# First loads of a batched matmul: one DMA of 8 KB runs for each operand in place of a 2 KB and a 6 KB one

## The chip, the cores and the metric

One core of a Trainium2 chip. The metric is the device time of one launch in microseconds. "Engine" in this document mostly means one of the core's 16 DMA engines; PE, DVE, ACT and SP are the tensor, vector, scalar and sync engines. HBM is the chip's large memory, SBUF the core's working memory, and PSUM holds what PE has summed. A DMA is moved in packets, and "2 KB runs" are stretches of 2 KB that lie together on both sides, one packet each; a run that is timed is one execution. A spread is the highest time less the lowest.

## The reference

```python
batch, m, k, n = 16, 512, 512, 512
a: [batch, k, m] float32      b: [batch, k, n] float32
out = np.matmul(a.transpose(0, 2, 1), b)      # float32
```

33.55 MB come in and 16.78 MB go out.

## The kernel before

Inputs come from HBM into four 2 MB buffers, are cast to bf16 by DVE, multiplied by PE, copied out of PSUM by ACT, and go back to HBM from seven 2 MB output buffers. Loads and stores are all issued by SP, in one order. Batches go in pairs, but the first pair is loaded batch by batch, so that the first matmuls need only 2 MB.

```python
in0_v = [x.rearrange("batch (p r) m -> batch p r m", r=RV) for x in (a, b)]       # RV = 4: 8 KB runs
top_v = [x[0][0:P].rearrange("p m -> p () m") for x in (a, b)]                    # 2 KB runs
low_v = [x[0][P:K].rearrange("(p r) m -> p r m", r=RV - 1) for x in (a, b)]       # 6 KB runs
...
for j in range(2):                                        # first a, first b
    nc.sync.dma_start(x_ts[j][:, 0:1, :], top_v[j]).then_inc(s_f[j], 16)
    nc.sync.dma_start(x_ts[j][:, 1:RV, :], low_v[j]).then_inc(s_f[j], 16)
for j in range(2):                                        # second a, second b
    nc.sync.dma_start(x_ts[j][:, RV:R, :], in0_v[j][1]).then_inc(s_x[j], 16)
for n in range(2, 2 * pairs):                             # all other loads, 2 MB each
    if n >= NX:
        nc.sync.wait_ge(s_in, n - NX + 1)                 # a buffer is free again
    ...
# DVE, first pair
for u in range(G):
    if u:
        nc.vector.wait_ge(s_mm, H)
    for j, bf_ts in enumerate((abf_ts, bbf_ts)):
        nc.vector.wait_ge(s_x[j] if u else s_f[j], 16 if u else 32)
        nc.vector.tensor_copy(out=bf_ts[0][:], in_=x_ts[j][:, u * RV:(u + 1) * RV, :]).then_inc(s_cast, 1)
```

The cast waits for 32 counts: both pieces of a tensor.

Of the kernel before, what the change touches and what calls it, by code (L numbers as in the profile page):

```python
# [8 lines left out]
def kernel(  # L9
# [6 lines left out]
    nc = tc.nc  # L16
    P = 128
    batch, K, M = a.shape
# [11 lines left out]
    RV = R // V  # L30
# [3 lines left out]
    in_v = [x.rearrange("(pair g) (q r) m -> pair (g q) r m", g=G, r=R) for x in (a, b)]  # L34



    in0_v = [x.rearrange("batch (p r) m -> batch p r m", r=RV) for x in (a, b)]
    top_v = [x[0][0:P].rearrange("p m -> p () m") for x in (a, b)]
    low_v = [x[0][P:K].rearrange("(p r) m -> p r m", r=RV - 1) for x in (a, b)]  # L40
    out_v = out.rearrange("(pair g) (c t) n -> pair c g t n", g=G, t=T)

    NX = 4
# [10 lines left out]
    x_ts = [pool.tile([P, R, M], f32, name=f"x{j}") for j in range(NX)]  # L54
# [5 lines left out]
    s_x = [tc.alloc_semaphore(f"s_x{j}") for j in range(NX)]  # L60
    s_f = [tc.alloc_semaphore(f"s_f{j}") for j in range(2)]
# [9 lines left out]

    with tc.tile_critical(no_gpsimd_drain=True):  # L72
        for j in range(2):
            nc.sync.dma_start(x_ts[j][:, 0:1, :], top_v[j]).then_inc(s_f[j], 16)
            nc.sync.dma_start(x_ts[j][:, 1:RV, :], low_v[j]).then_inc(s_f[j], 16)
        for j in range(2):
            nc.sync.dma_start(x_ts[j][:, RV:R, :], in0_v[j][1]).then_inc(s_x[j], 16)
        for n in range(2, 2 * pairs):
            if n >= NX:
                nc.sync.wait_ge(s_in, n - NX + 1)  # L80
            src, x = in_v[n % 2][n // 2], x_ts[n % NX]
# [11 lines left out]
        for u in range(G):  # L93
            if u:
                nc.vector.wait_ge(s_mm, H)
            for j, bf_ts in enumerate((abf_ts, bbf_ts)):
                nc.vector.wait_ge(s_x[j] if u else s_f[j], 16 if u else 32)
                nc.vector.tensor_copy(  # L98
                    out=bf_ts[0][:], in_=x_ts[j][:, u * RV:(u + 1) * RV, :]
                ).then_inc(s_cast, 1)  # L100
                if u == G - 1:
                    nc.vector.memset(dve_done[:, j:j + 1], 0.0).then_inc(s_in, 1)  # L102
# [120 lines left out]
```

## Time and profile before

| | |
|---|---|
| time, median of 3 runs | 123.50 us (123.36 to 123.52) |
| the execution that was profiled | 123.84 us, span 122.1 us |
| bytes moved | 50.33 MB |
| steady rate of the transfers | 427 to 430 GB/s |

The page and the windows of before are shown in the prediction. One thing is added here, the timeline of before at the first two casts (start, length, engine, line, operation; in brackets how long DVE had been idle and what ended it):

```profile
5.82 1.23 DVE L98 CAST abf<-x 128x2048 bf16<-128x2048 f32 x1 [5.82 <-DMA x<-in_a_dram]
8.95 1.23 DVE L98 CAST bbf<-x 128x2048 bf16<-128x2048 f32 x1 [1.91 <-DMA x<-in_b_dram]
```

The bracket of the second says that b's landing released it. So 8.95 us is when the first b was seen to be there.

A second source is used all through: the trace's packet records, with start, duration and size of every DMA packet. Each DMA ends with one 4-byte packet on each of the 16 engines, the semaphore increment. Sorted by time, 16 at a time, they tell when the first and when the last engine got through each DMA. The records do not name the engine: "the last engine" is whichever came last.

### The profile page before, as it was taken

What the parts mean: (1) busy time and instruction counts of PE and PEld (TensorE: products, weight loads), DVE (VectorE), ACT (ScalarE), POOL (GpSimd) and SP (SyncE); (2) the same over time, 40 slices, a digit from 0 to 9 for tenths busy, and PEclk for the clock granted to TensorE, in tenths of its full rate; (3) what the DMA queues carried; (4) which work ended last, traced back from release to release, by engine and by line L of the source; (5) the groups of instructions that cost most, each with busy time, mean ns of one, the idle gap of its engine ahead of it and who ended that gap; (6) DMA issues with size and microseconds to landing.
All of it is one profiled execution on the core that took longest, in us unless ns stands there. A gap on an engine that the chain in (4) does not pass through costs nothing.

```text
span 122.1 us, 1209 instructions
## 1 busy us (share of the span) xinstructions
PE 62.1 (51%) x480; PEld 35.0 (29%) x480; DVE 38.1 (31%) x48; ACT 32.2 (26%) x41; POOL 0.2 (0%) x4
## 2 busy tenths in 40 slices
PE   0005928379969749979919928989900000000000
PEld 0002304035546325636606605646500000000000
DVE  0033070680494092474356437492000000000000
ACT  4000332400570840091470290091570000000000
POOL 0000000000000000000000000000000000000000
PEclk9999999959999985999999999999997555555555
DMA  2999999999999999999999999999999999999993
GB/s 86 375 411 429 454 429 435 435 440 435 429 429 429 429 429 429 429 429 435 429 429 435 429 429 416 421 429 427 427 421 429 427 429 427 429 429 424 427 429 145
DMA packets 5200, 50.33 MB, mean 412 GB/s; under 512 B 464, under 2 KB 464, under 8 KB 976
## 3 DMA queue, kind: packets, MB, share of 16 engines
q1 hardware_dynamic: 5200, 50.33, 97.3%
HBM read 33.55 MB, written 16.78 MB: 412 GB/s over the span
## 4 chain that ended last, share of the span: by engine, by line
DMA 43%; DVE 7%; ACT 3%; PE 3%; issue 3%; ACTq 0%
DMA x<-in_b_dram 37%; DMA out_dram<-o 6%; DVE abf L117 4%; ACT o L180 3%; DVE bbf L117 3%; PE ps L135 3%; DVE done L123 0%; ACTq L72 0%
## 5 line engine op out<-in xcount | busy, mean ns | idle before, releaser
L155 PE MATMUL ps<-bbf,abf 64*128 64x512 bf16 x448 | 52.9, 393 | 13.1 <-PEq L150 13.1
L155 PEld LDWEIGHTS ps<-bbf,abf 64*128 64x128 bf16 x448 | 31.2, 113 | 34.8 <-issue 20.0
L180 ACT COPY o<-ps 128x1024 f32<-128x1024 f32 x28 | 26.3, 1026 | 40.5 <-PE ps L155 36.5
L117 DVE CAST abf<-x 128x2048 bf16<-128x2048 f32 x14 | 17.1, 1224 | 17.4 <-PE ps L155 13.3
L117 DVE CAST bbf<-x 128x2048 bf16<-128x2048 f32 x14 | 17.1, 1225 | 14.2 <-DMA x<-in_b_dram 14.2
L135 PE MATMUL ps<-bbf,abf 128*128 128x512 bf16 x32 | 9.2, 451 | 13.2 <-PEq L133 13.2
L135 PEld LDWEIGHTS ps<-bbf,abf 128*128 128x128 bf16 x32 | 3.8, 123 | 18.1 <-issue 16.1
L174 ACT COPY o<-ps 128x1024 f32<-128x1024 f32 x4 | 4.1, 1014 | 17.2 <-PE ps L135 17.2
L98 DVE CAST abf<-x 128x2048 bf16<-128x2048 f32 x2 | 2.5, 1227 | 11.7 <-PE ps L135 5.9
L98 DVE CAST bbf<-x 128x2048 bf16<-128x2048 f32 x2 | 2.5, 1225 | 1.9 <-DMA x<-in_b_dram 1.9
L185 ACT ACTIVATE done<-done 1x1 uint32<-1x1 uint32 x8 | 1.6, 196 | 0.0
L174 ACT ACT_TABLE_LOAD x1 | 1.3, 1283 | 0.9 <-SPq L72 0.9
L123 DVE MEMSET done<- 1x1 f32 x14 | 0.8, 59 | 0.0
L102 DVE MEMSET done<- 1x1 f32 x2 | 0.1, 59 | 0.0
L207 POOL MEMSET const-bfloat16-1.0<- 128x1 bf16 x1 | 0.1, 102 | 0.0
L207 POOL MEMSET const-uint8-127<- 128x1 uint8 x1 | 0.1, 102 | 0.0
L207 POOL MEMSET const-float32-0.0<- 128x1 f32 x1 | 0.1, 99 | 0.2 <-issue 0.2
L207 POOL MEMSET const-float32-1.0<- 128x1 f32 x1 | 0.1, 99 | 0.0
## 6 DMA issues: line engine op xcount, KB each, us to landing
out_dram<-o SPq DMA_DIRECT2D x8, 2048.0 KB, 21.8
x<-in_a_dram SPq DMA_DIRECT2D x7, 2048.0 KB, 12.1
x<-in_b_dram SPq DMA_DIRECT2D x6, 2048.0 KB, 15.9
x<-in_b_dram SPq DMA_DIRECT2D x3, 1024.0 KB, 13.4
x<-in_a_dram SPq DMA_DIRECT2D x1, 1024.0 KB, 8.6
x<-in_a_dram SPq DMA_DIRECT2D x1, 768.0 KB, 4.4
x<-in_b_dram SPq DMA_DIRECT2D x1, 768.0 KB, 6.6
x<-in_a_dram SPq DMA_DIRECT2D x1, 256.0 KB, 2.8
```

The lines of the kernel that those rows point to most:

```text
L98: nc.vector.tensor_copy(out=bf_ts[0][:], in_=x_ts[j][:, u * RV:(u + 1) * RV, :]).then_inc(s_cast, 1)
L102: nc.vector.memset(dve_done[:, j:j + 1], 0.0).then_inc(s_in, 1)
L117: nc.vector.tensor_copy(out=(bbf_ts if n % 2 else abf_ts)[v][:], in_=x_ts[n % NX][:, v * RV:(v + 1) * RV, :],).then_inc(s_cast, 1)
L123: nc.vector.memset(dve_done[:, n:n + 1], 0.0).then_inc(s_in, 1)
L135: mm = nc.tensor.matmul(ps_ts[0][h][:, t % 2, :], a_m[:, r, t], bbf_ts[0][:, r, :], start=(r == 0), stop=(r == RV - 1),)
L155: mm = nc.tensor.matmul(ps_ts[g][h][:, t % 2, :], a_m[:, t], bbf_ts[v][rows, r, :], start=(v == 0 and r == 0), stop=(v == V - 1 and r == R ...
L174: nc.scalar.copy(out=o_ts[0][:, g, 2 * h:2 * h + 2, :], in_=ps_ts[0][h][:]).then_inc(s_ev[h], 1)
L180: ev = nc.scalar.copy(out=o_ts[i % NO][:, g, 2 * h:2 * h + 2, :], in_=ps_ts[g][h][:])
L185: nc.scalar.memzero(act_done[:, i:i + 1]).then_inc(s_out, 1)
L207: nc = _bacc.Bacc("TRN2", target_bir_lowering=False, num_devices=1)
```

## The change

Its intent: fewer and longer packets at the very start, two DMAs fewer, two increments fewer.

```diff
-    top_v = [x[0][0:P].rearrange("p m -> p () m") for x in (a, b)]
-    low_v = [x[0][P:K].rearrange("(p r) m -> p r m", r=RV - 1) for x in (a, b)]
 ...
         for j in range(2):
-            nc.sync.dma_start(x_ts[j][:, 0:1, :], top_v[j]).then_inc(s_f[j], 16)
-            nc.sync.dma_start(x_ts[j][:, 1:RV, :], low_v[j]).then_inc(s_f[j], 16)
+            nc.sync.dma_start(x_ts[j][:, 0:RV, :], in0_v[j][0]).then_inc(s_f[j], 16)
 ...
-                nc.vector.wait_ge(s_x[j] if u else s_f[j], 16 if u else 32)
+                nc.vector.wait_ge(s_x[j] if u else s_f[j], 16)
```

## The prediction

> **What bounds the kernel now.** I read the page first (busy shares, the 40 slices, the DMA packets), then the waits of the DMA-issuing engine, then tables of short windows over the start and the end, then the timeline of the first 24 us, and last the trace's own packet records.
>
> The page: no compute engine is busy even 55% of the span, the DMA engines are.
>
> ```profile
> span 122.1 us, 1209 instructions
> PE 62.1 (51%) x480; PEld 35.0 (29%) x480; DVE 38.1 (31%) x48; ACT 32.2 (26%) x41; POOL 0.2 (0%) x4
> ...
> DMA  2999999999999999999999999999999999999993
> ...
> DMA packets 5200, 50.33 MB, mean 412 GB/s; under 512 B 464, under 2 KB 464, under 8 KB 976
> q1 hardware_dynamic: 5200, 50.33, 97.3%
> ...
> x<-in_a_dram SPq DMA_DIRECT2D x1, 768.0 KB, 4.4
> x<-in_b_dram SPq DMA_DIRECT2D x1, 768.0 KB, 6.6
> ```
>
> The reader is to see a transfer stream with no hole in it: every slice but the first and last reads 9, and 97.3% is the whole span less about 2.2 us at the start and 1.6 us at the end. So the end is: when the stream starts, plus 50.33 MB at its rate, plus a tail. What the casts and matmuls do matters only if it makes the stream run dry. The packet counts also fit the program: 29 DMAs x 16 = 464 tiny packets (the semaphore increments), and 976 - 464 = 512 packets of 2 or 6 KB, which are the four DMAs of the change (4 x 128).
>
> The windows (length, then engines, granted clock, DMA share, GB/s):
>
> ```profile
> 2.00:2.50 0.50, 0.00 (x0) 0.00 (x0) 0.00 (x0) 0.18 (x1) 0.00 (x0) 1.00 0.45 98
> 2.50:3.50 1.00, 0.00 (x0) 0.00 (x0) 0.00 (x0) 0.00 (x0) 0.00 (x0) 1.00 0.98 342
> 3.50:5.00 1.50, 0.00 (x0) 0.00 (x0) 0.00 (x0) 0.00 (x0) 0.00 (x0) 1.00 1.00 416
> 5.00:6.50 1.50, 0.00 (x0) 0.00 (x0) 0.68 (x1) 0.00 (x0) 0.00 (x0) 1.00 1.00 350
> 6.50:8.00 1.50, 0.00 (x0) 0.00 (x0) 0.54 (x1) 0.00 (x0) 0.00 (x0) 1.00 1.01 421
> 8.00:12.00 4.00, 1.53 (x4) 0.59 (x5) 1.23 (x1) 0.00 (x0) 0.00 (x0) 1.00 1.02 428
> ...
> 40.00:79.00 39.00, 30.19 (x260) 18.34 (x258) 18.94 (x24) 15.28 (x20) 0.00 (x0) 0.96 1.01 430
> 81.00:120.00 39.00, 7.21 (x64) 4.29 (x64) 2.20 (x4) 5.70 (x8) 0.00 (x0) 0.65 1.01 427
> 120.00:120.50 0.50, 0.00 (x0) 0.00 (x0) 0.00 (x0) 0.00 (x0) 0.00 (x0) 0.50 0.28 115
> ```
>
> The last column is the case. The rate is 427 to 430 GB/s everywhere except at two dips, 342 and 350, and these are where the 2 KB runs of a (2.2 to 3.3 us) and of b (5.0 to 6.7 us) go through. The 6 KB runs read 416 and 421; the second batch's 8 KB runs, from about 8 us, already read 428. The DMA share stays at 1.00 in the dips: the engines are not idle, their packets are slow.
>
> **What the Trainium skill says.** (1) "DMA: Bandwidth & Descriptors", section "Why small descriptors are slow (HBM only)", gives each packet a fixed overhead, put at about 3 cycles. The trace agrees that there is a fixed part. Median packet times in its records are 84 ns for 2 KB, 234 for 6 KB, 309 for 8 KB, 611 for 16 KB: from 2 to 8 KB that is 225 ns for 6144 B, so 9 ns fixed and 0.0366 ns a byte, and 6 KB comes out at exactly 234. (2) The same page, "Why a DMA increments its semaphore by 16 and not by 1": every engine that takes part posts one increment after its data. The 464 agree, 9 ns each. (3) "Perfetto Trace Analysis", section "DMA Optimizations", says that splitting into smaller chunks may let some start sooner if the DMA engines are generally idle. Here they are not, and the cast waits for both pieces of the split (32 counts), so nothing in this kernel uses the earlier piece.
>
> **The change, part by part.** It removes four DMAs (two of 256 KB, two of 768 KB) and adds two of 1 MB in the same buffer space; the cast waits for 16 counts instead of 32. Row order inside batch 0 changes for a and b alike, so the sum over k is the same. Casts, matmuls, evictions, outputs: unchanged, at the same durations.
>
> *Issues.* The six first issues stand 0.94 to 3.27 us, 0.47 us apart. Two fewer lets all later ones leave 0.94 us sooner. Worth nothing by itself: the stream is fed from a queue that holds 8.4 MB by 4.7 us.
>
> *Packets.* Each of the 16 engines now moves 2 x 8 packets of 2 KB and 2 x 8 of 6 KB: 16 x 84 + 16 x 234 = 5088 ns, with 4 increments 5124. Then 16 x 309 + 2 x 9 = 4962 ns. Gain 0.16 us, on the path that sets the end, since each engine works through a fixed list.
>
> *Stalls around the short packets.* The 0.16 does not explain the dips. Between 2.5 and 3.5 us the shortfall against 428 is 86 KB, between 5.0 and 6.5 it is 117 KB, and in the two 6 KB windows 18 and 11 KB: 232 KB, or 0.54 us in the mean of the engines. The records show where: at the first 6 KB packets behind the 2 KB ones, around 3.0 us, five packets take 310 to 380 ns longer than their median, and around 5.6 to 5.9 us seven take 180 to 780 ns longer. At the change from one 8 KB DMA to the next, nothing like it: only a few packets 50 to 135 ns over.
>
> *The last engine.* The end is set by the slowest engine, so I follow the increments of each DMA from the first engine's to the last's: top of a 2.95 to 3.35 us, rest of a 4.95 to 5.44, top of b 5.64 to 6.70, rest of b 7.70 to 8.57, second a 10.16 to 11.02. From there on the lag of 0.86 us stays to the nanosecond through all reads, and is still 0.86 at the last increment (119.94 to 120.80). From 8.57 on the last engine thus runs at a fixed pace: 120.80 - 8.57 = 112.23 us, then 1.3 us to the span's end. The span is the last engine's finish of b plus 113.5 us.
>
> So what is wanted is that finish after the change. An 8 KB DMA takes an engine 2.453 us (second a: 8.57 to 11.02). The last engine to start has its first packet near 2.77 us, and a first packet takes some 0.24 us extra (up to 241 ns in the records). 2.77 + 0.24 + 2 x 2.453 = 7.92 us instead of 8.57: 0.65 us less, if no 8 KB packet stalls. If the same engine loses 0.2 us all the same, 0.45. The floor is the 0.16 of packet overhead.
>
> *Sum.* Mechanism alone: 0.16 to 0.65 us, middle about 0.5, so a time near 123.0 from 123.5.
>
> **The rivals.**
> (a) *A slower start with long first runs.* Short first packets may get the engines going sooner; somebody chose 2 KB runs ahead of 6 KB, and as the cast waits for both, nothing else in the kernel gives a reason for it. Against it: the last engine's first packet already comes 0.6 us behind the first one's, which no packet size explains, and the dips are at the short runs. If true, 123.5 to 123.9.
> (b) *The gain is lost behind a wait.* The stream could run dry where a buffer comes free. The issuing engine's waits:
>
> ```profile
> SPq L83 <- DVE done L102: 13.5, 2, 12.7
> SPq L91 <- DMA x<-in_b_dram: 12.6, 1, 12.6
> ```
>
> The first ends at 17.34 us, when the load in front of it still runs until 22.34 on the first engine; with 1.24 us from issue to first packet (0.94 to 2.18 at the start) there are 3.8 us to spare, and the chain to it starts with b's landing, which the change brings forward. The second ends at 79.5; outputs issued then can start at 80.75, just as the first engine is through with the last load at 80.73. Tight, but it is timed by the stream itself and moves along with it; if lag shrinks it gets looser. So this rival costs 0.0, at worst 0.2 us.
> (c) *The earlier start of the casts is worth more.* b's landing (8.95 us, the cast's start) would come about 0.65 sooner, but no compute lies at the end: the last output is issued at 90.84 and lands 30 us later in a queue that is full. Worth 0.
>
> **Range and chances.** The mechanism gives 122.85 to 123.35, middle 123.0; rival (a) at about one in four pulls up. I say 123.1, and 122.6 to 123.7 for 8 in 10: the low end allows 0.9 us, the whole lag of the last engine taken away; the high end a start that costs 0.2. Runs of before lie within 0.16 us, so this is readable. Two per cent is 2.47 us, more than the first 8.6 us can give at all (every engine starting at 2.18 and taking 4.91 us would be through at 7.09, 1.5 us sooner): faster 0.01, same 0.97, slower 0.02.
>
> **What would show it.** In the changed profile: 4912 packets (5200 - 256 - 32), with 432 under 512 B and 432 under 8 KB; two fewer issues; 420 GB/s or more in 3.5 to 8 us with no dip near 5 to 6.5; the cast of b starting near 8.3 instead of 8.95; outputs' last packets near 120.2 and a span near 121.6. The page's rate after 10 us unchanged at 427 to 430. I am wrong in the step "stalls" if a dip or slow packets of 8 KB appear in the first 8 us, wrong in the step "last engine" if b comes in earlier but the end doesn't move with it, and wrong altogether if the first packets come later than 2.2 to 2.8 us.

## The result

| | median | range | runs |
|---|---|---|---|
| before | 123.51 us | 123.36 to 123.54 | 4 |
| after | 123.34 us | 123.17 to 123.40 | 4 |

Ratio 0.9986, 95% interval 0.9969 to 1.0003: the same at 2%. A ratio is the mean time of one kernel's runs over that of the other's in the same rounds, so not quite the ratio of the medians.

The page of after, the lines that answer to those of before:

```profile
span 121.7 us, 1207 instructions
PE 65.0 (53%) x480; PEld 35.6 (29%) x480; DVE 38.0 (31%) x48; ACT 32.2 (26%) x41; POOL 0.2 (0%) x4
...
DMA  3999999999999999999999999999999999999993
...
DMA packets 4912, 50.33 MB, mean 414 GB/s; under 512 B 432, under 2 KB 432, under 8 KB 432
...
q1 hardware_dynamic: 4912, 50.33, 97.8%
...
x<-in_b_dram SPq DMA_DIRECT2D x4, 1024.0 KB, 12.1
x<-in_a_dram SPq DMA_DIRECT2D x2, 1024.0 KB, 6.8
```

4912 packets, 432 of them increments, none left between 512 B and 8 KB. The stream still has no hole. Then the same windows (last columns: granted clock, DMA share, GB/s):

```profile
2.00:2.50 0.50, 0.00 (x0) 0.00 (x0) 0.00 (x0) 0.18 (x1) 0.00 (x0) 1.00 1.26 180
2.50:3.50 1.00, 0.00 (x0) 0.00 (x0) 0.00 (x0) 0.00 (x0) 0.00 (x0) 1.00 0.50 213
3.50:5.00 1.50, 0.00 (x0) 0.00 (x0) 0.00 (x0) 0.00 (x0) 0.00 (x0) 1.00 1.02 426
5.00:6.50 1.50, 0.00 (x0) 0.00 (x0) 0.69 (x1) 0.00 (x0) 0.00 (x0) 1.00 1.03 431
6.50:8.00 1.50, 0.00 (x0) 0.00 (x0) 0.54 (x1) 0.00 (x0) 0.00 (x0) 1.00 1.04 437
8.00:12.00 4.00, 2.21 (x6) 0.88 (x7) 1.23 (x1) 0.00 (x0) 0.00 (x0) 1.00 1.01 426
...
40.00:79.00 39.00, 30.52 (x248) 17.47 (x246) 18.31 (x24) 15.27 (x20) 0.00 (x0) 0.91 1.00 430
```

From 3.5 us on it runs at full rate; the dip at 5.0 to 6.5 (350 GB/s before) is gone. The start, though, is worse: 213 GB/s from 2.5 to 3.5 us where before had 342. The engines' first packets start earlier than before's (1.96 to 2.21 us, before 2.18 to 2.50), but the records give them 0.79 to 1.29 us each in place of 0.31, so the first 8 KB are through near 3 us. The earlier start is not the change's doing: two later profiles of before start at 1.96 and 1.98. b's landing, in the timeline of after:

```profile
5.81 1.23 DVE L94 CAST abf<-x 128x2048 bf16<-128x2048 f32 x1 [5.81 <-DMA x<-in_a_dram]
8.26 1.23 DVE L94 CAST bbf<-x 128x2048 bf16<-128x2048 f32 x1 [1.22 <-DMA x<-in_b_dram]
```

a lands when it did (5.81 and 5.82), b 0.69 us sooner. The waits of the issuing engine, after, against the two of before:

```profile
SPq L79 <- DVE done L98: 14.5, 2, 13.7
SPq L87 <- DMA x<-in_b_dram: 12.6, 1, 12.6
```

The first is longer although b came sooner, because SP was done with its first issues 0.7 us earlier, and because PE's first 16 matmuls took 6.57 us in this execution and 5.55 in that of before, so the first refill left at 17.67 (before 17.34). It cost nothing here.

So the profiles differ by 0.4 us in span (122.1 to 121.7) and 0.69 us in b's landing, the times by 0.17 us. That gap is what the experiments are about.

### The profile page after: what moved, and what is told of

It is laid out like the page before. It is cut to its first block, busy times and chain, and to the rows that moved or that the text cites. A ratio compares the mean times of both kernels' runs of the same rounds, so it can differ in the third digit from the quotient of the medians.

```text
span 121.7 us, 1207 instructions
## 1 busy us (share of the span) xinstructions
PE 65.0 (53%) x480; PEld 35.6 (29%) x480; DVE 38.0 (31%) x48; ACT 32.2 (26%) x41; POOL 0.2 (0%) x4
## 2 busy tenths in 40 slices
DMA packets 4912, 50.33 MB, mean 414 GB/s; under 512 B 432, under 2 KB 432, under 8 KB 432
## 3 DMA queue, kind: packets, MB, share of 16 engines
q1 hardware_dynamic: 4912, 50.33, 97.8%
## 5 line engine op out<-in xcount | busy, mean ns | idle before, releaser
L131 PE MATMUL ps<-bbf,abf 128*128 128x512 bf16 x32 | 11.9, 554 | 12.5 <-PEq L129 12.5
L131 PEld LDWEIGHTS ps<-bbf,abf 128*128 128x128 bf16 x32 | 4.3, 138 | 19.6 <-issue 19.1
```

Source lines behind the costliest of these rows:

```text
L131: mm = nc.tensor.matmul(ps_ts[0][h][:, t % 2, :], a_m[:, r, t], bbf_ts[0][:, r, :], start=(r == 0), stop=(r == RV - 1),)
```

## The experiments

Theories. **P** (packets): only the fixed time of 16 packets and two increments for each engine went away. **S** (stalls): 2 KB runs stall in every execution, and the change removes some 0.4 us of that. **N**: noise. After the first four runs came **V**: a tensor cut into two DMAs lets single engines fall behind by an amount that varies from execution to execution; later told apart as **VC** (the count of DMAs does it), **VA** (the addresses do) and **V2** (b's cut alone does it).

Twelve runs, of nine kernels, were made in three calls, each call on a chip of its own, with other runs of before among them. The changed kernel was not in call 3, so there it is compared across calls. All were correct.

### Call 1: before and after again

Both unchanged; no diff.

> The kernel before, unchanged, timed against itself: a null, and a second profile of it. The first profile of before was taken in an execution of 123.84 us, 0.34 above its median, so it may show more loss than a usual run has. Theory S (stalls behind the 2 KB runs are what the change removes, 0.4 us of it): ratio 1.000, and the new profile again shows b's first 1 MB through on the last engine near 8.5 us, with slow first 6 KB packets. Theory P (only the fixed time per packet is removed, about 0.10 us): ratio 1.000, but the stalls are a matter of one execution, and the new profile has b through at 8.1 us or earlier.

> The changed kernel again, to narrow the interval (0.9969 to 1.0003 so far). Theory S: 0.9960 to 0.9975, that is 0.3 to 0.5 us. Theory P: per packet the streams of both traces pace at 0.0368 ns a byte plus 5.4 ns (8 KB every 306.6 ns, 16 KB every 607.8 ns); 16 packets less for each engine are 0.09 us and two increments less 0.02, so 0.11 us, ratio 0.9991. Theory N (nothing but noise): 1.000. All of them: first packets take about 1 us again, b is through at 7.5 to 7.9 us.

Measured: the copy of before 123.35 us (122.95 to 123.55), after 123.30 (123.14 to 123.48), the 11 other runs of before 123.72 (123.37 to 124.74). Ratios 0.9963 (0.9929 to 0.9998) and 0.9957 (0.9925 to 0.9990). The null test thus failed: the same kernel against itself came out as much faster as the change did. In the mean the copy and after differ by 0.03 us. From this call alone nothing can be said of the change, and a ratio here has to be read with the spread of before in mind. The span in the trace of the copy of before is 121.55 us, and b was through on the last engine at 8.03 us, not 8.57. That missed the mark of S (8.5) and met that of P (8.1 or earlier), only just, and showed that the first profile was not a typical execution. Of after it was expected that first packets take about 1 us again: they took 0.31 to 0.39 us.

### Call 1: two DMAs of 4 KB runs

```diff
-    top_v = [x[0][0:P].rearrange("p m -> p () m") for x in (a, b)]
-    low_v = [x[0][P:K].rearrange("(p r) m -> p r m", r=RV - 1) for x in (a, b)]
+    top_v = [x[0][0:2 * P].rearrange("(p r) m -> p r m", r=2) for x in (a, b)]
+    low_v = [x[0][2 * P:K].rearrange("(p r) m -> p r m", r=2) for x in (a, b)]
```

(and row ranges 0:2 and 2:RV; this is made from before, so the cast waits for both)

> First a and b in two DMAs each, but of 4 KB runs both: the same number of DMAs, packets (32 for each engine) and increments as before, with no 2 KB packet. Theory P: as before, ratio 1.000 (within 0.0004). Theory S: no short packet, no stall, so most of the change's gain stays: 0.997 to 0.998, and no packet over 1.5 times its median behind the first of each engine.

Measured: 124.15 us (123.46 to 124.74), ratio 1.0034 (0.9992 to 1.0077), 0.85 us over after in the same call, with a spread of 1.3 us. Both theories missed: as many packets as before and no short one, yet slower than either kernel, and with single packets up to 810 ns over their median of 159 where S expected none. This is what theory V was made for.

### Call 1: one DMA of 2 KB runs

```diff
+    quarter_v = [x[0].rearrange("(r p) m -> p r m", r=RV) for x in (a, b)]
 ...
-            nc.sync.dma_start(x_ts[j][:, 0:RV, :], in0_v[j][0]).then_inc(s_f[j], 16)
+            nc.sync.dma_start(x_ts[j][:, 0:RV, :], quarter_v[j]).then_inc(s_f[j], 16)
```

> First a and b in one DMA each of 2 KB runs (64 packets for each engine in place of 16, the 6 KB ones gone). Against the changed kernel: theory P, 48 packets x 5.4 ns = 0.26 us more, so 0.15 us over before, ratio 1.0012. Theory S: 2 KB packets run 342 to 350 GB/s in the dips of before, which would make 2.1 MB take 6.1 us in place of 4.9, so 1.1 to 1.2 us more than after, ratio 1.006 to 1.008 to before.

Measured: 123.92 us (123.76 to 124.02), ratio 1.0011 (0.9978 to 1.0043); 0.62 us over after. By the ratio P was met, but the baseline of that call was high; against after, 0.62 is between P (0.26) and S (1.1). In its records b's 1 MB takes 2.57 us on the first engine and 2.60 on the last, where 8 KB runs take 2.45. That is 0.12 to 0.15 us for each tensor, far from S's rate of 350 GB/s. The rest, some 0.35 us, is lost before a is through (5.91 us on the last engine, after 5.42, less 0.13 for packets). Why that start is slower is open. Its spread is narrow: 0.26 us.

### Call 2: after and before, once more

> The changed kernel, now with a copy of before among the same runs (in the last call a copy of before came out 0.37% faster than the runs it was compared with, which is as much as is looked for; copies in one call are to be compared with each other). Theory P (packets, 0.11 us): mean 0.1 us under the copy of before. Theory S (stalls behind 2 KB runs in every execution): 0.3 to 0.5 under. Theory V (a DMA cut in two lets single engines fall behind by a varying amount): 0 to 0.3 under, and a narrower spread of times than before has (last call: 0.34 against 0.60 us).

> The kernel before, unchanged, in the same call as the changed one; ratio to the other runs of before 1.000 within 0.004 on all theories. Its profile: theory S has slow 6 KB packets at 5.6 to 6 us again and a lag of the last engine near 0.86 us; theory V has a lag between 0.4 and 1.3 us, another one than 0.86 and 0.58 of the two profiles so far; theory P has no view.

Measured: after 123.22 us (123.17 to 123.33), the copy of before 123.49 (123.06 to 123.88), the other runs of before 123.47 (123.19 to 123.91). Ratios 0.9980 (0.9961 to 0.9999) and 1.0007 (0.9983 to 1.0031). This time the null held, and after is 0.26 us under the copy in the mean. The spreads are 0.16 and 0.82 us. The profiled execution of before happened to be its fastest (123.06 us); in it there is no dip at 5.0 to 6.5 us:

```profile
5.00:6.50 1.50, 0.00 (x0) 0.00 (x0) 0.89 (x1) 0.00 (x0) 0.00 (x0) 1.00 1.07 423
```

423 where the first profile of the same kernel had 350. The lag of its last engine is 0.26 us (b through at 7.52 to 7.78), under V's range of 0.4 to 1.3, but a third value after 0.87 and 0.58. So S falls in its form "the same stall in every execution": the dip at b is not in each. Slow packets are, though. Over 100 ns above their median in the first 6.5 us are 20, 26 and 25 packets in the three profiles of before; here they stand around a's runs (2.14 to 3.27 us) and only three at b.

### Call 2: 4 KB runs, two DMAs against one

The slow two-DMA kernel again, unchanged, and the same 4 KB runs, to the same places, in one DMA:

```diff
+    half_v = [x[0].rearrange("(h p r) m -> p h r m", h=2, r=2) for x in (a, b)]
 ...
-            nc.sync.dma_start(x_ts[j][:, 0:RV, :], in0_v[j][0]).then_inc(s_f[j], 16)
+            nc.sync.dma_start(x_ts[j][:, 0:RV, :].rearrange("p (h r) m -> p h r m", h=2), half_v[j]).then_inc(s_f[j], 16)
```

> The two DMAs of 4 KB runs once more, which came out at 124.15 us (123.46 to 124.74) where theory P had the time of before and theory S less. If that was the chip: the mean of the copy of before within 0.15 us. Theory V: again 0.5 us or more over the changed kernel, with a spread of 0.8 us or more, and an engine that sits idle between 4.5 and 6 us.

> The same rows in the same 4 KB runs in the same places, but one DMA for a and one for b (32 packets for each engine, two increments in place of four). Theory P: 16 x 5.4 ns = 0.09 us over the changed kernel. Theory V: as the changed kernel within 0.15 us, with a narrow spread (0.4 us or less), as there is no second DMA. If the 4 KB runs themselves are what is slow: near the two-DMA version, 0.5 us or more over the changed kernel.

Measured: two DMAs 124.26 us (123.55 to 124.41), ratio 1.0042 (1.0013 to 1.0072); one DMA 123.30 us (123.19 to 123.44), ratio 0.9986 (0.9966 to 1.0006). Same rows, same runs, same packets but for two increments on each engine: 0.77 us apart in the mean, spread 0.86 against 0.25. In windows, first two DMAs, then one:

```profile
3.50:5.00 1.50, 0.00 (x0) 0.00 (x0) 0.00 (x0) 0.00 (x0) 0.00 (x0) 1.00 1.10 396
5.00:6.50 1.50, 0.00 (x0) 0.00 (x0) 0.98 (x1) 0.00 (x0) 0.00 (x0) 1.00 0.94 246
```

```profile
3.50:5.00 1.50, 0.00 (x0) 0.00 (x0) 0.00 (x0) 0.00 (x0) 0.00 (x0) 1.00 1.03 421
5.00:6.50 1.50, 0.00 (x0) 0.00 (x0) 0.74 (x1) 0.00 (x0) 0.00 (x0) 1.00 1.01 415
```

246 against 415 GB/s, where b begins. The records show 19 packets 260 to 770 ns over their median of 159 between 4.8 and 6.0 us, where b's first DMA begins, in the two-DMA kernel only. V's idle engine was there in the first profile of this kernel (0.12 us in the mean of the engines between 5.0 and 5.5) and hardly in this one (0.02): here the engines were waiting with a packet in hand. So it is not the 4 KB run length that costs; it is the cut, with what comes with it. For the cut changes the order too: as the patterns read, the one DMA takes a partition's two runs one after the other, and the two DMAs take all runs of the first half before any of the second. The traces hold no addresses, and no run here tells the number of DMAs from the order of the packets.

### Call 3: two DMAs on the changed kernel's own addresses

```diff
-            nc.sync.dma_start(x_ts[j][:, 0:RV, :], in0_v[j][0]).then_inc(s_f[j], 16)
+            nc.sync.dma_start(x_ts[j][:, 0:2, :], in0_v[j][0][:, 0:2, :]).then_inc(s_f[j], 16)
+            nc.sync.dma_start(x_ts[j][:, 2:RV, :], in0_v[j][0][:, 2:RV, :]).then_inc(s_f[j], 16)
 ...
-                nc.vector.wait_ge(s_x[j] if u else s_f[j], 16)
+                nc.vector.wait_ge(s_x[j] if u else s_f[j], 16 if u else 32)
```

> Four first DMAs of 4 KB runs as in the slow two-DMA version, but each takes every other 4 KB of the same 1 MB, so that a partition's rows and the engines' strides in HBM are those of the changed kernel. Theory VC (the lag comes from having two DMAs where one would do, whatever their addresses): 0.5 us or more over the changed kernel, that is 123.8 to 124.3, with a spread of 0.8 us. Theory VA (it comes from the addresses that the engines read side by side): 123.2 to 123.5 with a spread of 0.4 or less, packets costing 0.11 us.

Measured: 124.35 us (124.29 to 124.44), ratio 1.0068 (1.0054 to 1.0082). VA expected at most 123.5 and falls: the engines' strides in HBM are those of the changed kernel and it is slower by 1.1 us than after in the other calls. VC's time is met (0.5 us or more over after; 124.35 is just above its 123.8 to 124.3); its wide spread is not, these five runs lie within 0.15 us. So a cut's cost can be steady as well. The order of the packets is changed here too, as in the kernel above, so it stays a rival of the number. Windows:

```profile
5.00:6.50 1.50, 0.00 (x0) 0.00 (x0) 0.32 (x1) 0.00 (x0) 0.00 (x0) 1.00 1.01 347
6.50:8.00 1.50, 0.00 (x0) 0.00 (x0) 0.91 (x1) 0.00 (x0) 0.00 (x0) 1.00 1.04 369
```

### Call 3: only a cut

```diff
+            if j == 0:
+                nc.sync.dma_start(x_ts[j][:, 0:1, :], in0_v[j][0][:, 0:1, :]).then_inc(s_f[j], 16)
+                nc.sync.dma_start(x_ts[j][:, 1:RV, :], in0_v[j][0][:, 1:RV, :]).then_inc(s_f[j], 16)
+            else:
                 nc.sync.dma_start(x_ts[j][:, 0:RV, :], in0_v[j][0]).then_inc(s_f[j], 16)
```

(and the cast of a waits for 32)

> Only a is cut into a DMA of 2 KB runs and one of 6 KB (strided, so that rows agree with b), b comes in one DMA of 8 KB runs. In the profiles of before the slow packets stand where b's 2 KB DMA is, around 5.7 us, and two executions of before at 122.95 and 123.06 us were faster than any of the changed kernel (123.14). Theory V2 (a's short first runs start sooner, b's cut brings the lag): 123.0 to 123.2 and a spread under 0.4 us. Theory VC (each cut brings lag): between the two kernels, 123.3 to 123.4, spread 0.5. Theory P: 0.05 us over the changed kernel.

Measured: 124.27 us (123.80 to 125.13), ratio 1.0075 (1.0040 to 1.0110). This was the try at a version that beats both, and it is slower than both, outside all three expectations: not V2 (123.0 to 123.2), not VC's 123.3 to 123.4, not P. The 256 KB of a's 2 KB runs were through at 2.62 us on the first engine and at 4.52 on the last, and the window shows it:

```profile
2.50:3.50 1.00, 0.00 (x0) 0.00 (x0) 0.00 (x0) 0.00 (x0) 0.00 (x0) 1.00 0.80 160
```

It also tells against "so much for each cut": before cuts both tensors and loses less. Its 2 KB runs lie side by side in HBM, here they lie 8 KB apart. Whether that is the reason was not tested.

### Call 3: all loads in 2 KB packets

```diff
-    x_ts = [pool.tile([P, R, M], f32, name=f"x{j}") for j in range(NX)]
+    x_ts = [pool.tile([P, R, M + 8], f32, name=f"x{j}")[:, :, 0:M] for j in range(NX)]
```

> The changed kernel with 32 bytes of padding behind each row in the input tiles, so that all loads go in 2 KB packets, from the same HBM addresses, in the same DMAs: 1024 packets for each engine in place of 152. Theory P: 872 x 5.4 ns = 4.7 us more, about 128.0 us (with the 9 ns of the packet records in place of the pace: 7.8 us, 131.1). Theory S (2 KB runs go at 350 GB/s as in the dips of the first profile): 33.55 MB take 95.9 in place of 78.0 us, about 141 us.

Measured: 131.29 us (131.12 to 131.30), ratio 1.0625 (1.0610 to 1.0639). The page shows that the padding did what was wanted:

```profile
span 129.6 us, 1207 instructions
...
DMA packets 18864, 50.33 MB, mean 389 GB/s; under 512 B 432, under 2 KB 432, under 8 KB 16816
```

Against before in the same call the mean is 7.75 us more, for 1024 - 168 = 856 packets more on each engine: 9.05 ns a packet. That is the 9 ns which the prediction took from packet durations, and not the 5.4 ns that I had meanwhile drawn from the pace of 8 and 16 KB packets. And S's 141 us is far off: in a steady stream 2 KB packets run at 391 to 395 GB/s, not 350.

### Call 3: the first b cast later

```diff
             for j, bf_ts in enumerate((abf_ts, bbf_ts)):
+                if not u and j:
+                    nc.vector.wait_ge(s_x[0], 16)
```

> The changed kernel with the cast of b's first part made to wait for a's second part as well, so the first matmuls start some 2.2 us later (b's cast near 10.5 in place of 8.3 us). If the end hangs on the stream alone: as the changed kernel, 123.2 to 123.35 us, with a narrow spread. If the landing of b and the compute behind it matter: up to 2.2 us more, and a hole in the DMA share where the first freed buffer is refilled, near 22 us.

Measured: 123.65 us (123.34 to 123.80), ratio 1.0003 (0.9988 to 1.0017); mean 123.60, some 0.3 us over after in the other calls. The cast started at 10.74 us, 2.48 later. A small price is there, and not near 22 us, where the hole was expected. The load of the fourth pair's a (n = 6), in the timeline, and the windows around it:

```profile
30.36 0.33 SPq L79 DMA_DIRECT2D x<-in_a_dram  x1
```

```profile
30.00:31.50 1.50, 1.50 (x18) 0.99 (x16) 1.45 (x4) 0.00 (x0) 0.00 (x0) 1.00 0.99 426
31.50:33.00 1.50, 1.50 (x18) 0.99 (x16) 0.00 (x0) 0.00 (x0) 0.00 (x0) 1.00 1.00 350
33.00:34.50 1.50, 1.50 (x18) 0.99 (x16) 1.34 (x2) 0.00 (x0) 0.00 (x0) 1.00 1.05 448
```

The load before it was through on the first engine at 31.84 us, 1.48 us behind this issue, and that lead was too short: 350 GB/s for 1.5 us, about 0.3 us lost. In the records that load took the last engine 5.19 us, every other full load 4.86. In the changed kernel the same issue leaves at 27.95 and the stream needs it at 31.87, a lead of 3.9 us. So compute is off the path that sets the end, as predicted, with an estimated 2.1 us to spare (the issue came 2.41 us later and lost 0.3); take more than that and it comes back.

### All profiles side by side

From the packet records, in us. b is the first 1 MB of b. The padded kernel is left out, as its whole stream has another pace.

```
kernel                    b through, first / last engine   span     span - last
before (first profile)    7.70 / 8.57                      122.10   113.53
before (call 1)           7.45 / 8.03                      121.55   113.52
before (call 2)           7.52 / 7.78                      121.31   113.53
after (first profile)     7.52 / 7.88                      121.65   113.77
after (call 1)            7.09 / 7.88                      121.73   113.85
after (call 2)            7.60 / 7.89                      121.43   113.54
4 KB, two DMAs (call 1)   7.38 / 8.66                      122.15   113.49
4 KB, two DMAs (call 2)   7.69 / 9.02                      122.52   113.50
4 KB, two, strided        7.80 / 9.08                      122.57   113.49
4 KB, one DMA             7.70 / 7.88                      121.47   113.59
2 KB, one DMA             7.74 / 8.51                      122.03   113.52
only a cut                7.69 / 8.82                      122.45   113.63
b's cast later            7.49 / 7.95                      122.01   114.06
```

The last column is the reading that carries the case. In ten of thirteen profiles it lies within 0.14 us, 113.49 to 113.63, whatever the first loads were: the kernel ends 113.5 us after the last engine is through with the first b. The other three lost something later. In the first profile of after the last engine fell 0.2 us further behind between 85.8 and 90.9 us; in the second the last engine lost 0.34 us between 32 and 52 us; the third, b's later cast, has the hole told above and ends 1.5 us after its last increment where the others take 1.3. What slowed the two of after there was not looked into.

## Why the prediction was right, and where its size was off

Predicted 123.1 us (122.6 to 123.7), measured 123.34, in the range, and the same at 2% as given at 0.97. The range also holds before's own 123.51, so being in it says little for the mechanism; that has to be read from the steps.

Size first. Over calls 1 and 2 and the first result, before has 38 runs, mean 123.55 us and standard deviation 0.31; after has 16, mean 123.28 and 0.09. That is 0.27 us, with a standard error of about 0.06 if the runs are taken as independent; by call it is 0.17, 0.32 and 0.26. But 22 of the 38 are the other runs of before, and in call 1 these lay 0.45 us over the copy of the same kernel. Copy against copy, the fair comparison, the calls give 0.03 and 0.26; with the first result's 0.17 that is 0.15 us over 16 and 16 runs, again with a standard error of about 0.06. So the gain lies somewhere between 0.15 and 0.27 us, and the predicted 0.4 was one and a half times to nearly three times as much. N is unlikely on these figures, and no call alone would have told.

- **Transfer-bound, the end set by the last engine, span = its finish of b + 113.5 us**: shown, in the table above. The finish of b on it was predicted at 7.92 us and came at 7.88, 7.88 and 7.89; b's cast near 8.3 came at 8.26; the span near 121.6 came at 121.65, 121.73 and 121.43. Packet counts as predicted. Two of these hits are luck. 7.92 was built on a last engine that starts at 2.77 us and loses 0.24 on its first packet; in the records of before the sixteenth engine starts at 2.50, and the 0.24 belongs to second packets (the first took 81 to 116 ns). With 2.50 the same sum gives 7.65. What the three profiles of after share is the end of the slowest first packet, 3.27 to 3.28 us: the other seven at 306.6 ns and b's eight lead to 7.88. And the span: 7.92 and 113.5 make 121.4, not 121.6; the first two profiles come near 121.6 only by what they lost after 32 us.
- **Last engine, the step that was mis-sized**: the prediction took 8.57 us as what before has. That belonged to one execution, of 123.84 us where the median was 123.50, and the two later profiles had 8.03 and 7.78. Its first packet also came 0.2 us later than theirs (2.18, against 1.96 and 1.98). Had I asked whether the profiled execution was a usual one, the time table alone would have taken 0.34 off: 123.50 - 1.74 (time less span, 123.84 - 122.10) is a usual span of 121.76, so b is through at 8.24, and 8.24 - 7.92 gives 0.32 us in place of 0.65.
- **Stalls behind the 2 KB packets**: half right. The slow packets in the middle of a and b were real, and after's profiles have none at b. But the prediction's own sign against this step, slow packets of 8 KB in the first 8 us, came true: in the first profile of after all sixteen first packets took 482 to 982 ns over their median. In the mean of the engines the time over the medians in the first 12 us is 0.46, 0.52 and 0.48 us in before's profiles, 0.74, 0.15 and 0.46 in after's, so it did not clearly shrink; in after it stands in the first packets. And S, that short runs bring stalls each time, is refuted: 2 KB packets throughout run at 391 GB/s and more, with no packet 100 ns over its median after the first 3.5 us. 4 KB runs in two DMAs lose 0.8 us over the same runs in one. The cut into two DMAs, by their number or by the order of packets that comes with it, is what these runs point to: measured for 4 KB runs, and only inferred for before's 2 and 6 KB, since before's own run lengths were not tried in one DMA.
- **Packet overhead, 0.16 us**: the 9 ns a packet is confirmed at 9.05 in bulk. But it was called a floor, and it is none for a single execution: two runs of before (122.95 and 123.06 us) were faster than any of after's 16 (123.14 at best).
- **Rival (a), a slower start**: partly true, and in the profile of the second of those two it shows (the first was not profiled). The argument against it, a last engine that starts 0.6 us behind the first, was misread: 0.33 us. From 2.5 to 3.5 us after's three profiles have 213, 385 and 303 GB/s, before's 342, 305 and 346, so after's start varies and is not always the slower. Its last engine is through with a at 5.42 to 5.44 us each time, before's at 5.28 to 5.53. In before's profile of call 2 the last engine is through with b at 7.78 us, 0.1 us earlier than after's in any profile. I had given the rival a time of 123.5 to 123.9; where it shows it is a tenth of a microsecond, outweighed in the mean by what the cut costs.
- **Rival (b), lost behind a wait**: no hole opened in after. The spare time was given as 3.8 us at the first refill; the tighter place is two loads later, with about 2 us to spare.
- **Rival (c), earlier casts worth nothing**: shown in its own direction by the later cast, which lost only when a refill came too late.

Better said, then: the change does not so much speed the kernel up as make it steady. It trades a start that is sometimes 0.1 us faster for one that is through at 7.88 or 7.89 us in all three profiles, and takes the standard deviation of the time from 0.31 (0.24 with copies alone) to 0.09.

What stays open: why engines fall behind when one tensor comes in two DMAs. The packets concerned wait in the engine, in the 4 KB kernel mostly where the third DMA begins, with the same set of addresses as in a kernel that does not stall there, but in another order. The order itself, descriptors that come late for some engines, or engines that drift apart and then meet in HBM could each look like this; no run here tells them apart. Open too: why the cut of a alone, with runs 8 KB apart, loses more than before does with both cut, and why one DMA of 2 KB runs starts 0.35 us late. No version here beat the changed kernel.

## What to carry to other kernels

In a kernel that streams without holes, look for the last DMA engine, not the mean of them: in ten of thirteen profiles here a delay that it took in the first 9 us was still there at the end, within 0.14 us. Do not cut a load in two when nothing uses the first part, or time it both ways. And before a difference is read off one profile, hold the profiled execution's time against the median: here the profiled one lay 0.34 us above, more than the change was worth.

## What the Trainium skill lacked or had wrong

- "DMA: Bandwidth & Descriptors", "Why small descriptors are slow (HBM only)": puts the fixed cost on the engine's internal bus at about 3 cycles a packet without naming the clock, and adds 32 bytes of metadata for each operation. Measured 9.05 ns a packet in all (7.75 us for 856 more packets on each engine); at the 850 MHz that the page gives the fabric, 3 cycles would be an estimated 3.5 ns.
- The same page, "Latency and other measured facts": HWDGE first byte about 600 ns, without saying from where it counts. Here, in before and after, the first packet's record starts 1.0 to 1.25 us after the start of its issue (0.94 to 1.96 and 2.18); counted from the end of the issue (1.33) it is 0.63 to 0.85 us, near the page's figure. What the page lacks is how much a first packet varies: an 8 KB first packet took 0.79 to 1.29 us in one profile of the changed kernel, 0.31 to 0.39 in another.
- "Perfetto Trace Analysis", "DMA Optimizations": says when splitting a DMA may help, and in its point on splitting nothing of what it costs (another point has it that larger DMAs do better). Here two DMAs of 512 KB in place of one of 1 MB, for a and for b, cost 0.77 us (4 KB runs, same addresses, another order).
- No page has it that the last engine of a saturated stream does not catch up: in ten of thirteen profiles it took 112.2 to 112.3 us from its finish of b to its last increment, whether it lagged by 0.2 us at b or by 1.3; in the first profile of before the lag was 0.86 us from 11 us on to the end at 120.8.
